# Half the up-projection row tiles of five chunks per layer by a 2x2 block scheme of seven products

## The chip, the cores and the metric

The kernel runs on one core of one Trainium2 chip. The metric is device time in microseconds of one execution: 2205.43 us, the median of three runs (2205.32 to 2205.55). TensorE (PE) multiplies, VectorE (DVE) and ScalarE (ACT) do elementwise work, SyncE (SP) issues the weight loads, and GpSimd (POOL) does little here. SBUF holds the working data. TensorE writes its results to PSUM, which has eight banks of 512 fp32 columns for each of the 128 partitions.

## What is computed

The reference is a trunk of two encoder layers over 256 tokens of width 2048, in fp32. Each layer has a mixer (layer 0: pooling and attention, layer 1: mLSTM; neither is touched here) and then the gated feed-forward part, which the change is about:

```python
x = x + conv_ffn(rms_norm(x, norm_ffn[layer]), w_up[layer], conv_w[layer], conv_b[layer], w_down[layer])

def conv_ffn(x, w_up, conv_w, conv_b, w_down):
    u = x @ w_up                                   # 256 x 2048 times 2048 x 11264
    up = jnp.pad(u, ((0, 0), (1, 1), (0, 0)))
    c = conv_w.astype(u.dtype)
    u = c[0] * up[:, :-2] + c[1] * up[:, 1:-1] + c[2] * up[:, 2:] + conv_b.astype(u.dtype)
    gate, val = jnp.split(u, 2, axis=-1)           # 5632 columns each
    return (jax.nn.silu(gate) * val) @ w_down      # 5632 x 2048
```

## The kernel before

**Products.** Every fp32 operand is used as two TensorE operands: a high half (the value rounded to the type that TensorE multiplies) and a low half (the rest). A product takes three matmuls: high x high, high x low, low x high. `mm` (line 203) issues each.

**Weights.** All weights come through one `Stream`. A load (SP queue, line 80) brings a 128 x 1024 fp32 tile of 512 KB into one of six raw buffers; `split` then makes the high half with a ScalarE cast (line 89) and the low half with a VectorE subtraction (line 90) into one of four "hl" buffers. The stream loads five tiles ahead of the tile in use and splits two ahead. A raw buffer is free again after its subtraction, an hl buffer after the last matmul that reads it.

**Feed-forward layer** (`ffn_layer`). The 5632 gate columns are 44 row tiles of 128 (with the 44 value tiles beside them), in chunks `FCH` of 4, 8, 8, 8, 8, 8 row tiles. `up` computes one row tile with the weights as the stationary operand and the 256 tokens moving: for each of 16 K tiles two 512-wide and two 256-wide matmuls (`stat_part`), into one buffer of the PSUM pool "mm" (two buffers of two banks). Then `gather` copies the one part out on ScalarE (line 366) and adds the other on VectorE (line 367), the norm's row scale R is multiplied in (line 890), and the conv, silu, gate and the split of the result into the chunk's tile `g` follow (lines 894 to 903, here called the tail). After a chunk's row tiles, `down` of the chunk before runs: for each of four column blocks of 512 a sum over that chunk's K tiles, with the activations stationary and the weights moving (`mov_part`, 512 wide, three terms, two token halves), into an "mm" buffer; `residual` adds it to x on VectorE (line 376). The second PSUM pool "ps" (four buffers of one bank) serves transposes.

**Order.** TensorE's order is the order in which the program is written. ScalarE's, VectorE's and SP's instructions are ordered by a scheduler before the run, and each engine then works through its own list from front to back. Small jobs beside the main line (norms, transposes) are generators in `Weave`, `wv`, which runs them at due times counted in estimated TensorE time (`wv.tick`).

```python
mmp = pool("mm", 2, space=PSUM)          # 2 x [128, 2, 512]
psp = pool("ps", 4, space=PSUM)          # 4 x [128, 512]
st = Stream(nc, wp, sp, weights, 5, 2)   # six raw buffers, four hl buffers
```

## Time and profile before

| | |
|---|---|
| runs, median of 3 | 2205.43 us (2205.32 to 2205.55) |
| profiled execution, span from first to last instruction | 2203.1 us (2.3 us under the median of the runs; no other time is listed for it) |
| mean granted TensorE clock | 1.000 |
| TensorE busy | 2197.9 us, 100% |
| VectorE busy | 1525.5 us, 69% |
| ScalarE busy | 1169.0 us, 53% |
| low halves of weights on VectorE (line 90) | 772, mean 1218 ns |
| casts of weights on ScalarE (line 89) | 771, mean 1047 ns |
| HBM traffic | 415.71 MB, mean 189 GB/s |

How to read it: rows give busy time, the mean of one instruction in ns and the idle time of the engine just before, with what ended it. Matmul rows overlap, as they are pipelined, so the pace of TensorE is read from the chain of waits in order of time (so many matmuls in so many us) and not from the mean of a matmul. A stage row gives busy time and, in brackets, the number of instructions for each engine, then the granted clock, the share of DMA time and the rate. Line numbers are those of the kernel before.

### The profile page before, as it was taken

The numbers are of one execution on the slowest core, as the hardware profiler recorded it, in microseconds if no ns is written. First come the engines' busy times: TensorE is split into PE (matmuls) and PEld (weight loads), VectorE is DVE, ScalarE is ACT, GpSimd is POOL, SyncE is SP. The second block draws the span as 40 slices with busy tenths as digits, with TensorE's granted clock in tenths as the row PEclk, the third lists the DMA queues.
The fourth block names the chain that finished last, engine by engine and source line by source line (L and its number), as shares of the span: only waits on it lengthen the run. The fifth ranks groups of instructions, "written<-read, shape, count | busy, mean of one in ns | idle before, by whom it ended". The sixth has DMA issues, their size and how long they took to land.

```text
span 2203.1 us, 30458 instructions
## 1 busy us (share of the span) xinstructions
PE 2197.9 (100%) x11616; PEld 1883.7 (86%) x11616; DVE 1525.5 (69%) x2172; ACT 1169.0 (53%) x1664; POOL 28.1 (1%) x40
## 2 busy tenths in 40 slices
PE   9999999999999999999999999999999999999999
PEld 8888888888888888889888888888888888888887
DVE  7686677776776767666767676667777677676764
ACT  7665555554554545456555454555555455454542
POOL 0020000000000000000000000000000000000000
PEclk9999999999999999999999999999999999999999
DMA  9555556556565666656565555556555656555664
GB/s 323 179 164 170 175 191 187 190 189 198 184 194 188 192 191 191 196 171 205 162 202 177 185 181 171 186 177 191 186 191 189 197 185 193 189 191 191 192 191 144
DMA packets 118036, 415.71 MB, mean 189 GB/s; under 512 B 13082, under 2 KB 15426, under 8 KB 117890
## 3 DMA queue, kind: packets, MB, share of 16 engines
q1 hardware_dynamic: 114656, 409.76, 58.2%
q10 hardware_dynamic: 3074, 3.75, 0.6%
q8 instruction: 91, 1.49, 0.3%
q14 instruction: 55, 0.45, 0.1%
q0 software_dynamic: 160, 0.26, 0.0%
HBM read 411.58 MB, written 2.14 MB: 188 GB/s over the span
## 4 chain that ended last, share of the span: by engine, by line
PE 100%; DVE 0%; issue 0%
PE up L203 45%; PE dn L203 21%; PE op L203 8%; PE mv L203 4%; PE mq L203 4%; PE mk L203 4%; PE mo L203 4%; PE qproj L203 3%; PE pool L203 1%; PE kproj L203 1%; PE vproj L203 1%; PE qk L203 1%; PE av L203 1%; PE end L203 0%; PE xt L254 0%; PE sc L203 0%
## 5 line engine op out<-in xcount | busy, mean ns | idle before, releaser
L90 DVE TENSOR_TENSOR hl<-w,hl 128x1024 fp32r<-128x1024 f32 (+2 forms) x772 | 939.1, 1218 | 466.6 <-ACT hl L89 464.8
L89 ACT CAST hl<-w 128x1024 fp32r<-128x1024 f32 (+1 forms) x771 | 806.9, 1047 | 677.3 <-PE dn L203 242.1
L203 PE MATMUL up<-xx,hl 128*128 128x512 f32 (+1 forms) x5632 | 984.2, 337 | 0.0
L203 PEld LDWEIGHTS up<-xx,hl 128*128 128x128 f32 x5632 | 857.9, 188 | 125.9
L203 PE MATMUL dn<-hl,g 128*128 128x512 f32 x2064 | 471.3, 389 | 0.0
L203 PEld LDWEIGHTS dn<-hl,g 128*128 128x128 f32 x2064 | 386.2, 188 | 79.5
L366 ACT COPY tb_up<-up 128x512 f32<-128x512 f32 x88 | 51.7, 587 | 154.0 <-PE up L203 154.0
L367 DVE TENSOR_TENSOR tb_up<-up,tb_up 128x512 f32<-128x512 f32 x88 | 60.8, 691 | 97.0 <-ACT tb_up L366 97.0
L894 ACT ACTIVATE y<-tb_up,cst 128x256 f32<-128x256 f32 x176 | 96.4, 595 | 47.0 <-DVE tb_up L890 47.0
L203 PE MATMUL mk<-xx,hl 128*128 128x512 f32 (+1 forms) x512 | 92.2, 337 | 0.0
L203 PE MATMUL mq<-xx,hl 128*128 128x512 f32 (+1 forms) x512 | 92.1, 337 | 0.0
L203 PE MATMUL mv<-hl,xx 128*128 128x512 f32 (+2 forms) x480 | 91.7, 350 | 0.0
L203 PE MATMUL op<-hl,cat 128*128 128x512 f32 x384 | 91.6, 393 | 0.0
L203 PE MATMUL mo<-hl,xx 128*128 128x512 f32 x384 | 90.4, 391 | 0.0
L203 PE MATMUL op<-hl,mcat 128*128 128x512 f32 x384 | 89.5, 392 | 0.0
L203 PEld LDWEIGHTS mq<-xx,hl 128*128 128x128 f32 x512 | 79.2, 188 | 11.6
L203 PEld LDWEIGHTS mk<-xx,hl 128*128 128x128 f32 x512 | 79.0, 188 | 11.4
L203 PEld LDWEIGHTS mv<-hl,xx 128*128 128x128 f32 x480 | 78.3, 189 | 11.2
L203 PEld LDWEIGHTS op<-hl,mcat 128*128 128x128 f32 x384 | 71.5, 188 | 14.6
L203 PEld LDWEIGHTS mo<-hl,xx 128*128 128x128 f32 x384 | 71.0, 188 | 14.2
L203 PEld LDWEIGHTS op<-hl,cat 128*128 128x128 f32 x384 | 70.9, 188 | 14.1
L895 DVE SCALAR_TENSOR_TENSOR y<-tb_up,cst,y 128x255 f32<-128x255 f32 x176 | 76.8, 478 | 0.0
(209 smaller groups left out, 1270.4 us busy)
## 6 DMA issues: line engine op xcount, KB each, us to landing
w<-in_up SPq DMA_DIRECT2D x352, 512.0 KB, 3.6
w<-in_dn SPq DMA_DIRECT2D x176, 512.0 KB, 4.1
w<-in_m_in SPq DMA_DIRECT2D x124, 512.0 KB, 4.1
w<-in_a_in SPq DMA_DIRECT2D x46, 512.0 KB, 4.4
w<-in_a_out SPq DMA_DIRECT2D x32, 512.0 KB, 3.4
w<-in_m_out SPq DMA_DIRECT2D x32, 512.0 KB, 3.5
w<-in_m_g SPq DMA_DIRECT2D x5, 432.0 KB, 3.4
x<-in_xn SPq DMA_DIRECT2D x4, 512.0 KB, 9.5
```

What stands on the lines that cost most here:

```text
L89: (self.nc.vector.tensor_copy if i + c == 0 else self.nc.scalar.copy)(hl[:, 0, c : c + n], w[:, c : c + n])
L90: self.nc.vector.tensor_sub(hl[:, 1, c : c + n], w[:, c : c + n], hl[:, 0, c : c + n].bitcast(F32))
L203: pe.matmul(out_, lhsT, rhs, start=start, stop=stop, skip_group_check=True)
L366: a.copy(tb, ps[:, :, 1, :])
L367: v.tensor_add(tb, ps[:, :, 0, :], tb)
L894: a.activation(y[:, j, :], u[:, j, :], AF.Identity, scale=cw(tl, 1), bias=cw(tl, 3))
L895: v.scalar_tensor_tensor(y[:, j, 1:S], u[:, j, 0 : S - 1], cw(tl, 0), y[:, j, 1:S], ALU.mult, ALU.add)
```

## The change

In chunks 1 to 5 of each layer (the five with eight row tiles), the last four of the eight row tiles are no longer computed one by one. With their value tiles they are 1024 output columns; these, the 256 tokens and each pair of K tiles are cut in two, so that each K pair is a 2x2 by 2x2 block product. Instead of eight block products of [128 tokens x 128] by [128 x 512] it takes seven, of sums of blocks: four activation sums (`sums`, once per layer, on VectorE from the already split activations) and weight sums made in `split` on VectorE in the raw buffers. The seven products are collected over the eight K pairs in six PSUM banks: one "mm" buffer (products 1 and 2 in the first bank, 3 in the second) and all four "ps" buffers. Weight tiles come in threes per K pair: "base", "one" (to which VectorE adds base) and "two" (whose halves VectorE adds to half of one and to each other), each feeding two products; four plain tiles per scheme finish the first output block. `decode` combines the banks on VectorE and ScalarE, `finish` transposes the result back to row tiles with TensorE and goes on with the unchanged tail. Per scheme 28 weight tiles are loaded and split where 16 were.

`_ffn_plan` writes TensorE's order by hand: row tiles in quarters, down blocks in slots of two K tiles, and the scheme's steps of one weight tile (six matmuls) between them. Down blocks of the chunk before now run between the row tiles of the chunk. From the feed-forward layer's start to its end the stream has one more raw and one more hl buffer, loads seven tiles ahead and splits three ahead.

```diff
+    def home(self, i, raw):
+        if self.more is None or i >= self.more[2]:
+            return self.wpool if raw else self.spool
+        return ((self.wpool if i % 7 < 6 else self.more[0]) if raw else
+                (self.spool if i % 5 < 4 else self.more[1]))
 
     def load(self, pieces=1):
         i = self.n_load
-        width = self.srcs[i].shape[-1]
+        src = self.srcs[i]
+        kind, src = src if isinstance(src, tuple) else ("plain", src)
+        width = src.shape[-1]
         n = width // pieces
-        w = self.wpool.tile([P, CH * P], F32, tag="w", name=f"w{i}")
+        w = self.home(i, True).tile([P, CH * P], F32, tag="w", name=f"w{i}")
         for c in range(0, width, n):
-            self.nc.sync.dma_start(w[:, c : c + n], self.srcs[i][:, c : c + n])
-        self.w[i] = w, n, width
+            self.nc.sync.dma_start(w[:, c : c + n], src[:, c : c + n])
+        self.w[i] = w, n, width, kind
         self.n_load += 1
 
     def split(self, then=None):
         i = self.n_split
-        w, n, width = self.w.pop(i)
-        hl = self.spool.tile([P, 2, CH * P], F32R, tag="hl", name=f"hl{i}")
+        w, n, width, kind = self.w.pop(i)
+        hl = self.home(i, False).tile([P, 2, CH * P], F32R, tag="hl", name=f"hl{i}")
+        if kind == "base":
+            self.base = w
+        if kind == "one":
+            self.one = w
+            self.nc.vector.tensor_add(w, w, self.base)
+        if kind == "two":
+            self.nc.vector.tensor_add(w[:, 0:512], w[:, 0:512], self.one[:, 0:512])
+            self.nc.vector.tensor_add(w[:, 512:1024], w[:, 512:1024], w[:, 0:512])
         for c in range(0, width, n):
             (self.nc.vector.tensor_copy if i + c == 0 else self.nc.scalar.copy)(hl[:, 0, c : c + n], w[:, c : c + n])
             self.nc.vector.tensor_sub(hl[:, 1, c : c + n], w[:, c : c + n], hl[:, 0, c : c + n].bitcast(F32))
...
-            def up(f, gt, i):
-                ps = stat_group(xx, list(range(KT)), f"up{layer}_{f}")
-                wv.until(lambda: norm.R is not None)
-                u = gather(tp, ps, f"up{layer}_{f}")
-                v.tensor_mul(u, u, bc(norm.R, 2))
...
+            def up(f, gt, i):
+                ps = mmp.tile([P, 2, 2, S], F32, tag="mm", name=f"up{layer}_{f}")
+                for q in range(KT // 4):
+                    stat_part(ps, xx, list(range(4 * q, 4 * q + 4)), q == 0, q == KT // 4 - 1)
+                    if q < KT // 4 - 1:
+                        yield
+                wv.until(lambda: norm.R is not None)
+                u = gather(tp, ps, f"up{layer}_{f}")
+                v.tensor_mul(u, u, bc(norm.R, 2))
+                tail(u, f, gt, i)
+
+            def sums():
+
+                vv = actp.tile([P, 2, KT // 2, S], F32, tag="B1", name=f"v{layer}")
+                for h in range(2):
+                    ks = slice(8 * h, 8 * h + 8)
+                    v.tensor_add(vv[:, 0], norm.xx[:, ks, 0, :].bitcast(F32), norm.xx[:, ks, 1, :].bitcast(F32))
+                    yield 5.0
+                    q = vv[:, 0].rearrange("p (a k) (t c) -> p a k t c", k=2, t=2)
+                    a11, a21, a12, a22 = (q[:, :, k, t, :] for k in range(2) for t in range(2))
+                    raw = vv[:, 1].rearrange("p k s -> p (k s)").rearrange("p (j a c) -> p j a c", j=4, a=4)
+                    s1, s2, s3, s4 = (raw[:, j] for j in range(4))
+                    v.tensor_sub(s1, a21, a22)
+                    v.tensor_add(s3, a11, a21)
+                    yield 3.0
+                    v.scalar_tensor_tensor(s2, s1, -1.0, a11, ALU.mult, ALU.subtract)
+                    v.tensor_sub(s4, s3, a12)
+                    v.tensor_sub(s4, s4, a22)
+                    yield 4.0
+                    for j in range(4):
+                        hi, lo = (sx[:, j, 4 * h : 4 * h + 4, i, :] for i in range(2))
+                        a.copy(hi, raw[:, j])
+                        v.tensor_sub(lo, raw[:, j], hi.bitcast(F32))
+                        yield 2.0
+
+            def product(bank, act, w, c, first, last):
+
+                (xh, xl), (wh, wl) = act, (w[:, j, c : c + 512] for j in range(2))
+                mm(bank, xh, wh, first, False)
+                mm(bank, xh, wl, False, False)
+                mm(bank, xl, wh, False, last)
+                wv.tick(0.68)
+
+            def block_of(k, t):
+                return [norm.xx[:, k, j, t * P : t * P + P] for j in range(2)]
+
+            def sum_of(j, p):
+                return [sx[:, j, p, i, :] for i in range(2)]
+
+            def quads(fs, gt, i0, name):
+
+                banks = {}
+                m = KT // 2
+                for p in range(m):
+                    ends = p == 0, p == m - 1
+                    for k in range(3):
+                        hl = st.next()
+                        if p == 0:
+                            if k == 0:
+                                two = mmp.tile([P, 2, 512], F32, tag="mm", name=f"p13_{name}")
+                                banks[1], banks[3] = two[:, 0], two[:, 1]
+                            else:
+                                for j in ((5, 7), (6, 4))[k - 1]:
+                                    banks[j] = psp.tile([P, 512], F32, tag="ps", name=f"p{j}_{name}")
+                        left = ((1, block_of(2 * p, 0)), (3, sum_of(3, p))), \
+                            ((5, sum_of(0, p)), (7, sum_of(2, p))), ((6, sum_of(1, p)), (4, block_of(2 * p + 1, 1)))
+                        for n, (j, act) in enumerate(left[k]):
+                            product(banks[j], act, hl, n * 512, *ends)
+                        if p == m - 1 and k == 0:
+                            c12 = cp1.tile([P, 512], F32, tag="c12", name=f"c12_{name}")
+                            a.copy(c12, banks[1])
+                        if p == m - 1 and k == 2:
+                            c12, c21, c22 = decode(banks, c12, name)
+                            wv.add(finish(c12, c22, fs[2:], gt, i0 + 2, name), 7.0)
+                        yield
+                for p in range(0, m, 2):
+                    hl = st.next()
+                    for n in range(2):
+                        product(banks[1], block_of(2 * (p + n) + 1, 0), hl, n * 512, False, p + n == m - 1)
+                    if p == m - 2:
+                        c11 = cp1.tile([P, 512], F32, tag="c11", name=f"c11_{name}")
+                        a.activation(c11, banks[1], AF.Copy, scale=norm.rcol[:, 0:1])
+                        wv.add(finish(c11, c21, fs[:2], gt, i0, name), 4.0)
+                    yield
+
+            def decode(banks, c12, name):
+
+                r1 = norm.rcol[:, 1:2]
+                c21 = cp1.tile([P, 512], F32, tag="c21", name=f"c21_{name}")
+                c22 = cp1.tile([P, 512], F32, tag="c22", name=f"c22_{name}")
+                v.tensor_add(c12, c12, banks[6])
+                v.tensor_add(c21, c12, banks[7])
+                a.activation(c21, c21, AF.Copy, scale=r1)
+                a.activation(c12, c12, AF.Copy, scale=n0)
+                v.scalar_tensor_tensor(c12, banks[3], n0, c12, ALU.mult, ALU.add)
+                v.scalar_tensor_tensor(c12, banks[5], n0, c12, ALU.mult, ALU.add)
+                v.scalar_tensor_tensor(c22, banks[5], r1, c21, ALU.mult, ALU.add)
+                v.scalar_tensor_tensor(c21, banks[4], r1, c21, ALU.mult, ALU.subtract)
+                return c12, c21, c22
+
+            def finish(top, bottom, fs, gt, i0, name):
+
+                for n, f in enumerate(fs):
+                    tr = psp.tile([P, 2, S], F32, tag="ps", name=f"tr{layer}_{f}")
+                    for j in range(2):
+                        for t, src in enumerate((top, bottom)):
+                            c = (2 * j + n) * P
+                            pe.transpose(tr[:, j, t * P : t * P + P], src[:, c : c + P], ident)
+                    u = tp.tile([P, 2, S], F32, tag="tb", name=f"tb_{layer}_{f}")
+                    a.copy(u, tr)
+                    tail(u, f, gt, i0 + n)
+                    yield 2.5
...
+            def down(c, gt, b):
...
+                for k in range(0, len(kts), 2):
+                    mov_part(ps, lambda k: gt[:, k], kts[k : k + 2], k == 0, k == len(kts) - 2)
+                    if k < len(kts) - 2:
+                        yield
+                residual(ps, b)
...
+            wv.add(sums_ready(), 8.0)
+            st.la, st.sa, st.more = 7, 3, (lp(f"fw{layer}", 1), lp(f"fh{layer}", 1), st.at + len(_ffn_plan()))
+            gts, run = {}, {}
+            for step in _ffn_plan():
+                kind, c = step[:2]
+                if kind != "d" and c not in gts:
+                    gts[c] = actp.tile([P, 8, 2, S], F32R, tag=f"B{c % 2}", name=f"g{layer}_{c}")
+                key = step[:3]
+                if key not in run:
+                    f0 = sum(FCH[:c])
+                    run[key] = (up(f0 + step[2], gts[c], step[2]) if kind == "n" else
+                                down(c, gts[c], step[2]) if kind == "d" else
+                                quads([f0 + 4 + j for j in range(4)], gts[c], 4, f"{layer}_{c}"))
+                next(run[key], None)
+            for e in run.values():
+                assert next(e, None) is None
+            st.la, st.sa, st.more = 5, 2, None
...
+def _ffn_plan():
+
+    plan = []
     for c, n in enumerate(FCH):
-        seq += [("u", u + i) for i in range(4 * n)]
-        u += 4 * n
+        whole = n - 4 if c else n
+        fill = [("n", c, i) for i in range(whole)]
         if c:
-            m = FCH[c - 1] // 4 * 8
-            seq += [("d", d + i) for i in range(m)]
-            d += m
-    m = FCH[-1] // 4 * 8
-    seq += [("d", d + i) for i in range(m)]
+            down = [("d", c - 1, b) for b in range(NB)]
+            fill = fill[:2] + down[:1] + fill[2:3] + down[1:2] + fill[3:] + down[2:]
+        slots = []
+        for e in fill:
+            slots += [e] * (4 if e[0] == "n" else FCH[e[1]] // 2)
+        if not c:
+            plan += slots
+            continue
+        m, late = KT // 2, c == len(FCH) - 1
+        here = [[] for _ in slots]
+        if c > 1:
+            for k in range(4):
+                here[k + 1].append(("s", c - 1, 0))
+        first, end = (0, len(slots)) if c == 1 else (8, len(slots)) if not late else (6, 24)
+        for k in range(3 * m):
+            here[first + k * (end - first) // (3 * m)].append(("s", c, 0))
+        if late:
+            for k in range(4):
+                here[end + k].append(("s", c, 0))
+        for e, extra in zip(slots, here):
+            plan += [e] + extra
+    for b in range(NB):
+        plan += [("d", len(FCH) - 1, b)] * (FCH[-1] // 2)
+    return plan
...
+def _quad_chunks(w):
+
+    out = []
+    for c in range(1, len(FCH)):
+        f = sum(FCH[:c]) + FCH[c] - 4
+        t = w.reshape(KT // 2, 2, P, 2, FT, P)[:, :, :, :, f : f + 4]
+        t = t.reshape(KT // 2, 2, P, 2, 2, 2, P).transpose(0, 1, 4, 2, 3, 5, 6).reshape(KT // 2, 2, 2, P, 512)
+        b11, b12, b21, b22 = (t[:, k, n] for k in range(2) for n in range(2))
+
+        def two(l, r):
+            return np.concatenate([l, r], axis=2)
+
+        out.append(np.stack([two(b11, b22), two(b12, b12), two(b22, b21)], axis=1))
+        out.append(two(b21[0::2], b21[1::2])[:, None])
```

71 lines of the change are left out of this document (43 added, 28 removed).

## The prediction, made before the run

> **What bounds the kernel now.** I read the page first, then the chain of waits in order of time, then one steady stretch of the feed-forward layer (eight up-projection row tiles and four down blocks) by engine, by group and instruction by instruction.
>
> The page: the span, busy time by engine, granted clock, traffic, the chain's share by engine.
>
> ```profile
> span 2203.1 us, 30458 instructions
> ...
> PE 2197.9 (100%) x11616; PEld 1883.7 (86%) x11616; DVE 1525.5 (69%) x2172; ACT 1169.0 (53%) x1664; POOL 28.1 (1%) x40
> ...
> PEclk9999999999999999999999999999999999999999
> ...
> DMA packets 118036, 415.71 MB, mean 189 GB/s; under 512 B 13082, under 2 KB 15426, under 8 KB 117890
> ...
> PE 100%; DVE 0%; issue 0%
> ```
>
> TensorE sets the time everywhere, at full clock. What a piece of it costs stands in the chain of waits (start, us, what):
>
> ```profile
> 1425.73 0.44 PE xt L254 x4
> ...
> 545.71 89.16 PE up L203 x512
> 634.87 43.53 PE dn L203 x192
> ```
>
> One up row tile is 89.16/8 = 11.145 us (64 matmuls, half of them 256 wide); a 512-wide matmul with the activation as weights is 43.53/192 = 0.2267 us; four transposes are 0.44 us.
>
> The same stretch by engine, then VectorE's groups and ScalarE's cast (busy, mean ns, idle before; the first row gives PE, PEld, DVE, ACT and POOL busy, clock, DMA share, GB/s):
>
> ```profile
> 545.70:678.40 132.70, 132.70 (x706) 113.85 (x705) 91.24 (x120) 68.02 (x88) 0.00 (x0) 1.00 0.60 191
> ...
> L90 DVE TENSOR_TENSOR hl<-w,hl 128x1024 fp32r<-128x1024 f32 x48 | 58.7, 1222 | 30.7 <-ACT hl L89 30.7
> L897 DVE SCALAR_TENSOR_TENSOR y<-tb_up,cst,y 128x255 f32<-128x255 f32 x16 | 7.0, 478 | 0.0
> ...
> L367 DVE TENSOR_TENSOR tb_up<-up,tb_up 128x512 f32<-128x512 f32 x8 | 5.5, 692 | 8.8 <-ACT tb_up L366 8.8
> L376 DVE TENSOR_TENSOR x<-x,dn 128x512 f32<-128x512 f32 x8 | 5.1, 684 | 1.6 <-PE dn L203 1.6
> ...
> L89 ACT CAST hl<-w 128x1024 fp32r<-128x1024 f32 x48 | 50.4, 1050 | 43.7 <-PE dn L203 23.6 <-PE up L203 20.1
> ```
>
> VectorE has 41.5 us of room in 132.7. Its instructions overlap a little at their ends, so I price them by the distance between starts, from the timeline (VectorE, then the one ScalarE row):
>
> ```profile
> 558.83 1.22 DVE L90 TENSOR_TENSOR hl<-w,hl 128x1024 fp32r<-128x1024 f32 x1
> 559.97 0.87 DVE L895 SCALAR_TENSOR_TENSOR y<-tb_up,cst,y 128x255 f32<-128x255 f32 x2
> 560.76 0.87 DVE L897 SCALAR_TENSOR_TENSOR y<-tb_up,cst,y 128x255 f32<-128x255 f32 x2
> ...
> 579.79 0.69 DVE L367 TENSOR_TENSOR tb_up<-up,tb_up 128x512 f32<-128x512 f32 x1 [1.10 <-ACT tb_up L366]
> 580.52 0.69 DVE L890 TENSOR_TENSOR tb_up<-tb_up,R 128x512 f32<-128x512 f32 x1
> 581.13 1.22 DVE L90 TENSOR_TENSOR hl<-w,hl 128x1024 fp32r<-128x1024 f32 x1
> ...
> 579.17 0.59 ACT L366 COPY tb_up<-up 128x512 f32<-128x512 f32 x1 [1.74 <-PE up L203]
> ```
>
> 1024 columns take 1.14 us, 512 take 0.61 (0.73 when the next one needs the result), two 255-column conv steps 0.79; a 256-column one I take at 0.34. The third up tile ends at 545.71 + 33.44 = 579.15; its bank pair is free when the add at 579.79 ends, 1.33 us later. Today nobody waits, since the other pair takes over.
>
> **The change, term by term.** *TensorE.* Ten times (five K chunks, two layers) four up row tiles go: 4 x 11.145 = 44.58 us. In come 8 K pairs x 7 products x 3 terms = 168 512-wide matmuls, 38.09, priced by the down rows since the operands stand the same way round, and 16 transposes to turn the result back, 1.76. Net -4.73 each, -47.3 us in all. Were nothing else to change, the profiled span would be 2203.1 - 47.3 = 2155.8; the runs lie 2.3 us above the span (2205.43 against 2203.1).
>
> *VectorE*, per chunk of that 132.7 us: 28 weight tiles in place of 16, so 12 more low halves at 1.14 = +13.7; eight sums "one" of 1024 columns, +9.1; eight "two" of 512 and, dependent, 512, 8 x 1.34 = +10.7; decoding, six operations of about 0.65, +4.0; four gathers and scalings gone, -5.3. 91.2 + 32.2 = 123.4 us against TensorE's new 128.0: from 69% to 96%. *ScalarE*: 12 more casts of 1.05 and a few copies, 68 + 15 = 83 us, no bound.
>
> *What becomes of PSUM.* The scheme holds one "mm" pair and all four "ps" banks from its first product to its decoding. An up tile or down block in between has only the other pair, and the next one may start only when VectorE has emptied it. Between two such groups TensorE has one scheme step of six matmuls, 1.36 us, which just covers the 1.33 us above, but only if VectorE stands ready. VectorE works in the order written into the program. That order, in the changed program, is what the following counts use; numbers are weight tiles.
>
> *First stretch of a middle chunk (third to fifth)*, from the residual add of the previous down column 3 to that of the new column 0. TensorE: 8 scheme steps 10.9, two up tiles 22.3, a down block of four slots 10.9, transposes 1.8: 45.9 us. VectorE must pass, ahead of that second residual: 20 low halves 22.8; a residual add 1.3; decoding 4.0; the tails of four scheme tiles 4 x 2.26 (two conv pairs, gate product, low half) and of two plain tiles 2 x 3.6 (with gather and scaling), 16.2; three "one" 3.4; two "two" 2.7: 50.4 us. So the next up tile, which needs the bank pair, is at least 4.5 us late, whatever lead the weights have.
>
> *Loads.* The order puts each "one" close behind the low half that frees its raw buffer (seven tiles before): for example tile 231's sum stands three 256-column operations and one low half (2.2 us) behind tile 224's low half. The load takes longer:
>
> ```profile
> DMA to landing us min/median/max: 3.3/3.7/4.5
> ```
>
> So VectorE, being late, also waits up to 1.5 us there. Walking the queue through one middle chunk with 3.8 us from release to landing gives TensorE waits of 0.8 (second up tile), 2.1 (first product of the new scheme) and 2.7 (the up tile after column 0): 5.6. The rest of the chunk has 82.1 us of TensorE against 70.4 of VectorE; there the walk leaves waits of 0.1 to 1.3 at four boundaries, 2.4. Together 8.0 per middle chunk, so 128.0 + 8.0 = 136 against 132.7.
>
> The Trainium skill, "DMA: Bandwidth & Descriptors", section "Anatomy of one DMA", fits 2.0 us plus bytes over 436 GB/s (for transfers GpSimd issues), an estimate of 3.2 us for these 512 KB. The row of this trace is longer and decides; by the page each of those waits would be about 0.5 us shorter and the total some 8 us lower.
>
> *Other chunks.* First chunk: the activation sums are two adds of 2048 columns (2.2 each), ten of 512 and eight low halves (0.61 each), 15.4 us, ahead of the first gather; with its other work VectorE reaches the weights of the third tile after about 27 us, TensorE after 23.4, less a small lead: 3 us. Second chunk: 97.6 us of TensorE, 90.6 of VectorE with fourteen sums to wait for, no first stretch: between 0 and 10; I take 5. Last chunk: the scheme starts two slots earlier, so the first stretch holds four low halves and one "two" more, 50.4 + 5.9 = 56.3 against 51.3 (four scheme steps more), then looser stretches: 5.0 at least, 9 taken. Attention, mLSTM and the last down chunk are untouched.
>
> *Sum.* Per layer 3 + 5 + 3 x 8 + 9 = 41 us of waits; two layers 82; 2203.1 - 47.3 + 82 + 2.3 = 2240 us. Bounds per layer: below 0 + 0 + 3 x 4.5 + 5 = 18.5 (VectorE's work alone), total 2195; above, the second rival.
>
> A page's rule speaks against the change by itself. The Trainium skill, "Perfetto Trace Analysis", section "Optimizing Tensor Performance", wants independent matmul groups to rotate through PSUM banks, so that emptying one overlaps the next. The 1.33 us row agrees on the cost, but the step between the groups covers it here unless VectorE is late; by the rule alone, eight uncovered boundaries a chunk would be 10.6 us, near the forecast.
>
> **The rivals.** *Slower than before is wrong: VectorE is not late.* Place: the residual add of each chunk's first down column. If the sums' loads land in time (VectorE's other waits use up the 1.5 us) and the leftovers of the previous stretch give it a lead, only the 4.5 and 5 us bounds stay: 2195. For it: VectorE's total is still under TensorE's, 123.4 to 128.0. Against: its order leaves 50.4 us to do in 45.9. It decides once that work fits 45.9, 9% less; then waits vanish and the time goes down to 2158 to 2165.
>
> *Loads slow down.* Each scheme adds 12 tiles of 0.524 MB, in all 415.7 + 62.9 = 479 MB, and in the dense stretches two tiles per 4.1 us, 256 GB/s. At the start of the run, where traffic is dense, a load lands late (rate, then kind and time to landing):
>
> ```profile
> DMA packets 6364, 17.58 MB, mean 352 GB/s; under 512 B 673, under 2 KB 801, under 8 KB 6361
> ...
> w<-in_a_in SPq DMA_DIRECT2D x23, 512.0 KB, 8.0
> ```
>
> Between 3.7 at 191 GB/s and 8.0 at 352, 256 gives 5.4. Then two sums of a first stretch wait 1.7 longer each and the looser stretches lose about 2: +5.4 per middle chunk, some 25 per layer, 2290. Against: those first loads queue many at a time, here at most a few are under way.
>
> *The change does less than it says:* the 512-wide products could take the up rows' time per column instead (11.145 us for 24,576 columns, 0.232 per 512): 39.0 per scheme, 9 us more in all, 2249, inside the forecast's range.
>
> **Chances.** Forecast, waits outgrow the saving (2210 to 2268): 0.62. Late only by VectorE's work, or not at all (2158 to 2201): 0.16. Slow loads (over 2268): 0.16. A tie, where the two cancel: 0.06. The measurement tells about 0.2%, 4.4 us, from no change: faster 0.16, same 0.06, slower 0.78. The likeliest gives 2240. The range reaches from VectorE's work bound, 2195, to where the slow loads begin to tell, 2280; it leaves out the wholly hidden case and the worst of the slow loads.
>
> **What would show it.** Right: VectorE at 90% or more in the middle chunks; TensorE with gaps of 2 to 3 us twice per chunk, ended by VectorE's residual add and gather; in the list of waits, weight sums waiting for loads; a middle chunk of about 136 us; transposes and products at 0.11 and 0.227 us each. Wrong: chunks near 128 us (VectorE was never late), gaps ended by casts or by DMA rather than by PSUM (then weights, not banks, are short), or a granted clock below 1.0.

## The result and the profile after

The changed kernel takes 2350.5 us (median of four runs, 2346.9 to 2356.9) against 2205.45: a ratio of 1.066, with an interval from 1.064 to 1.068. The direction was forecast, the size was not: +145 us against +35, and outside the range of 2195 to 2280.

From the page of the changed kernel, the lines that answer to those of before (span, busy time by engine, granted clock, traffic, the chain's share by engine):

```profile
span 2350.2 us, 29972 instructions
...
PE 2221.7 (95%) x10896; PEld 1846.9 (79%) x10896; DVE 1858.6 (79%) x2554; ACT 1323.7 (56%) x1840; POOL 29.2 (1%) x40
...
PEclk9999999999999999999999999999999999999899
...
DMA packets 135317, 478.59 MB, mean 204 GB/s; under 512 B 15002, under 2 KB 17346, under 8 KB 135170
...
PE 60%; DVE 20%; DMA 12%; issue 6%; ACT 2%; DVEq 0%; ACTq 0%
```

No engine is full: TensorE has gaps, VectorE is at 79%, and the chain, all TensorE before, now runs through VectorE and the loads for a third. The work is as counted. In the chain of the changed kernel, by time, a scheme step of six products and four transposes back (start, us, what):

```profile
571.32 1.37 PE p L220 x6
...
580.69 0.44 PE tr L1027 x4
```

The scheme itself is priced right (1.36 and 0.44 in the forecast). The loss lies in waits. The first feed-forward layer, cut at the residual add of each chunk's last down column (first chunk, second, third to fifth, last with the last down columns), by engine, then clock, DMA share and rate:

```profile
256.10:317.70 61.60, 50.94 (x283) 44.20 (x281) 52.36 (x80) 33.91 (x50) 0.71 (x1) 0.92 0.47 150
317.70:427.60 109.90, 101.03 (x476) 82.78 (x476) 92.35 (x114) 58.99 (x71) 0.00 (x0) 0.97 0.68 216
427.60:571.40 143.80, 133.39 (x634) 108.78 (x634) 121.56 (x155) 82.68 (x105) 0.00 (x0) 0.99 0.69 219
571.40:713.10 141.70, 133.02 (x633) 108.60 (x632) 121.22 (x154) 82.60 (x104) 0.00 (x0) 0.99 0.71 223
713.10:854.00 140.90, 132.99 (x633) 108.77 (x632) 121.67 (x154) 82.63 (x104) 0.00 (x0) 0.99 0.71 224
854.00:1059.10 205.10, 191.25 (x894) 156.42 (x893) 168.75 (x227) 122.80 (x171) 0.31 (x1) 0.98 0.64 202
```

Against TensorE's work alone (46.6, 97.6, three times 128.0, 182.8) these are 15, 12, 16, 14, 13 and 22 us too long: 92 in this layer and, by difference, 102 in the other. The forecast had 3, 5, 8, 8, 8 and 9. So no single place failed; every stretch loses 1.6 to 5 times what was allowed. In the second layer the middle chunks take 141.2, 145.5 and 145.1 us, 13 to 17.5 too long; the last two of them:

```profile
1848.30:1993.80 145.50, 134.65 (x633) 109.64 (x633) 121.94 (x155) 82.91 (x105) 0.00 (x0) 0.98 0.68 217
1993.80:2138.90 145.10, 134.87 (x633) 109.84 (x632) 121.59 (x154) 82.65 (x104) 0.00 (x0) 0.98 0.67 218
```

Who TensorE waits for, and VectorE for loads (the list of waits of the changed kernel, TensorE's rows and two of VectorE's: us in total, times, longest):

```profile
PE dn L220 <- DVE tb_up L384: 28.2, 22, 3.4
PE npr L220 <- DVE n L1086: 21.3, 2, 10.7
PE up L220 <- DVE x L393: 21.0, 15, 2.4
PE p L220 <- DVE tb_up L384: 14.9, 8, 2.6
PE up L220 <- DVE tb_up L384: 10.5, 10, 1.8
...
DVE w L101 <- DMA w<-in_qm: 61.2, 55, 4.6
...
DVE w L103 <- DMA w<-in_qm: 25.2, 29, 2.4
```

Lines 384 (gather) and 393 (residual add) are where VectorE empties the one PSUM pair left to plain groups: 74.6 us in these rows. The `npr` row is the norm of the feed-forward input, 10.7 us in each layer, which the forecast did not have. The last two rows are weight sums waiting for their own loads, 86.4 us. The middle chunk from 571 to 713, split where the forecast split it:

```profile
571.36:625.20 53.84, 49.23 (x243) 40.22 (x242) 50.18 (x76) 36.10 (x54) 0.00 (x0) 0.97 0.65 200
625.20:713.10 87.90, 83.83 (x392) 68.38 (x391) 71.08 (x80) 46.54 (x51) 0.00 (x0) 1.00 0.75 237
```

First stretch: VectorE busy 50.18 (50.4 counted), but 53.84 long (45.9 + 5.6 forecast). Rest: 87.90 (82.1 + 2.4). VectorE's work was right, its idle time and what follows from it was not.

And the clock drops. Around 606 us (windows of 3.4 us, same columns, clock before the DMA share; then TensorE's timeline):

```profile
605.30:608.70 3.40, 1.13 (x6) 0.59 (x4) 3.12 (x4) 2.40 (x5) 0.00 (x0) 0.99 0.42 143
608.70:612.10 3.40, 3.08 (x7) 2.48 (x8) 3.40 (x8) 0.14 (x1) 0.00 (x0) 0.50 0.56 170
612.10:615.50 3.40, 3.40 (x16) 2.77 (x15) 3.40 (x7) 2.86 (x5) 0.00 (x0) 1.00 0.50 155
```

```profile
603.54 2.89 PE L220 MATMUL dn<-hl,g 128*128 128x512 f32 x12
609.02 1.62 PE L220 MATMUL p<-hl,xx 128*128 128x512 f32 x3 [2.59 <-DVE tb_up L384]
```

A wait of 2.59 us ends at 609.02, and from 608.70 on TensorE has half speed for 3.4 us. The mean clock of the run is 0.980, or 47 us' worth of 2350; what that costs is asked below. Of the 194 us that TensorE loses, 123 are idle time; its busy time is 71 us longer than forecast (2221.7 us against 2197.9 - 47.3), which is where work at half speed would show. The Trainium skill, "TensorE: Matmul & The Clock Gate", section "HAM oscillation — how this bites in real kernels", warns of idle gaps over about 3.4 us. The half rate that it gives agrees with this trace (0.50), but here a wait of 2.59 us was enough, and half speed lasted 3.4 us where its example has about 1.67.

### The profile page after: what moved, and what is told of

Same layout as the page of the kernel before. It is cut to its first block, busy times and chain, and to the rows that moved or that the text cites. A ratio compares the mean times of both kernels' runs of the same rounds, so it can differ in the third digit from the quotient of the medians.

```text
span 2350.2 us, 29972 instructions
## 1 busy us (share of the span) xinstructions
PE 2221.7 (95%) x10896; PEld 1846.9 (79%) x10896; DVE 1858.6 (79%) x2554; ACT 1323.7 (56%) x1840; POOL 29.2 (1%) x40
## 4 chain that ended last, share of the span: by engine, by line
PE 60%; DVE 20%; DMA 12%; issue 6%; ACT 2%; DVEq 0%; ACTq 0%
PE dn L220 12%; DMA w<-in_qm 12%; DVE hl L107 10%; PE up L220 9%; PE op L220 7%; PE p L220 6%; PE mv L220 4%; PE mq L220 4%; PE mk L220 4%; PE mo L220 4%; PE qproj L220 3%; ACT hl L106 1%; DVE y L912 1%; DVE y L910 1%; DVE tb_up L384 1%
## 5 line engine op out<-in xcount | busy, mean ns | idle before, releaser
L106 ACT CAST hl<-w 128x1024 fp32r<-128x1024 f32 (+2 forms) x891 | 929.8, 1048 | 703.5 <-PE dn L220 191.2
L107 DVE TENSOR_TENSOR hl<-w,hl 128x1024 fp32r<-128x1024 f32 (+2 forms) x892 | 1077.7, 1218 | 287.7 <-ACT hl L106 280.8
L220 PE MATMUL up<-xx,hl 128*128 128x512 f32 (+1 forms) x3072 | 578.9, 343 | 35.7 <-DVE x L393 21.0
L220 PEld LDWEIGHTS up<-xx,hl 128*128 128x128 f32 x3072 | 495.2, 191 | 129.9 <-ACT hl L106 18.6
L220 PE MATMUL dn<-hl,g 128*128 128x512 f32 x2064 | 520.7, 404 | 42.4 <-DVE tb_up L384 28.2
L220 PEld LDWEIGHTS dn<-hl,g 128*128 128x128 f32 x2064 | 395.6, 194 | 146.8 <-DVE tb_up L384 35.1
L220 PE MATMUL p<-hl,sx 128*128 128x512 f32 x960 | 263.2, 398 | 0.0
L220 PE MATMUL p<-hl,xx 128*128 128x512 f32 x720 | 205.6, 402 | 23.7 <-DVE tb_up L384 14.9
L220 PEld LDWEIGHTS p<-hl,sx 128*128 128x128 f32 x960 | 177.9, 191 | 35.8
L220 PEld LDWEIGHTS p<-hl,xx 128*128 128x128 f32 x720 | 131.6, 191 | 51.7 <-issue 16.2
L101 DVE TENSOR_TENSOR w<-w,w 128x1024 f32<-128x1024 f32 x80 | 98.0, 1224 | 64.2 <-DMA w<-in_qm 61.2
L220 PE MATMUL mk<-xx,hl 128*128 128x512 f32 (+1 forms) x512 | 92.2, 337 | 0.0
L220 PE MATMUL mq<-xx,hl 128*128 128x512 f32 (+1 forms) x512 | 92.1, 337 | 0.0
L220 PE MATMUL mv<-hl,xx 128*128 128x512 f32 (+2 forms) x480 | 91.7, 350 | 0.0
L220 PE MATMUL op<-hl,cat 128*128 128x512 f32 x384 | 91.6, 393 | 0.0
L220 PE MATMUL mo<-hl,xx 128*128 128x512 f32 x384 | 90.4, 391 | 0.0
L220 PE MATMUL op<-hl,mcat 128*128 128x512 f32 x384 | 89.5, 392 | 0.0
L220 PEld LDWEIGHTS mq<-xx,hl 128*128 128x128 f32 x512 | 79.2, 188 | 11.6
L220 PEld LDWEIGHTS mk<-xx,hl 128*128 128x128 f32 x512 | 79.0, 188 | 11.4
L220 PEld LDWEIGHTS mv<-hl,xx 128*128 128x128 f32 x480 | 78.3, 189 | 11.2
L220 PEld LDWEIGHTS op<-hl,mcat 128*128 128x128 f32 x384 | 71.5, 188 | 14.6
L220 PEld LDWEIGHTS mo<-hl,xx 128*128 128x128 f32 x384 | 71.0, 188 | 14.1
```

The lines of the kernel that those rows point to most:

```text
L101: self.nc.vector.tensor_add(w, w, self.base)
L106: (self.nc.vector.tensor_copy if i + c == 0 else self.nc.scalar.copy)(hl[:, 0, c : c + n], w[:, c : c + n])
L107: self.nc.vector.tensor_sub(hl[:, 1, c : c + n], w[:, c : c + n], hl[:, 0, c : c + n].bitcast(F32))
L220: pe.matmul(out_, lhsT, rhs, start=start, stop=stop, skip_group_check=True)
```

## Experiments

Each kernel ran beside the kernel before on the same chip (medians of 2205.4 to 2205.6 us). Ratios are to that. A difference between two changed kernels compares medians of separate rounds, and the four runs of a kernel spread over 2 to 12 us, so a few us between two of them are not clear of noise. The kernels with an eighth raw buffer, with ScalarE emptying PSUM, and with sums that do not wait for loads also let the tile `c11` share the place of `c12`, to make room; what that costs was not measured.

**Activation sums behind the norm**

```diff
+ unit = xsp.tile([P, 1], F32, tag="unit", name=f"unit{layer}")
+ v.tensor_scalar(unit, norm.R[:, 0:1], 0.0, 1.0, ALU.mult, ALU.add)
...
- v.tensor_add(vv[:, 0], norm.xx[:, ks, 0, :].bitcast(F32), norm.xx[:, ks, 1, :].bitcast(F32))
+ v.scalar_tensor_tensor(vv[:, 0], norm.xx[:, ks, 0, :].bitcast(F32), unit,
+                        norm.xx[:, ks, 1, :].bitcast(F32), ALU.mult, ALU.add)
```

> The changed kernel, but the activation sums (sums) may start only once the norm's row scale R is there. What it tells apart: in the changed kernel the first up tile of layer 0 reaches its gather at 282.2 us against 269.3 before, 12.9 us late, with TensorE standing before the small matmul of the norm. If the activation sums stand ahead of the norm's chain in VectorE's order and cause it, that gather comes back to within 1 us of 269.3, the waits of that matmul (21 us in the two layers) go to nearly 0, and the time falls by 20 to 30 us to about 2325. If instead the sums are just too much work for the first chunk, wherever they stand, the 12.9 us appear again at the second or third tile and the time stays within 8 us of 2350.

2330.1 us, ratio 1.057 [1.055, 1.059]: 20 less. In the changed kernel VectorE's timeline has the sums (936 to 952) ahead of the operand that the norm needs (311):

```profile
257.48 2.28 DVE L936 TENSOR_TENSOR v<-xx 128x2048 f32<-128x2048 f32 x1
...
270.88 2.29 DVE L936 TENSOR_TENSOR v<-xx 128x2048 f32<-128x2048 f32 x1
...
276.23 0.48 DVE L311 TENSOR_SCALAR dg<-cst,re_n 128x128 f32<-128x128 f32 x2
```

With the edit TensorE runs through (timeline of this experiment):

```profile
265.90 0.60 PE L220 MATMUL npr<-dg,cst 128*128 128x256 f32 x2
266.15 34.02 PE L220 MATMUL up<-xx,hl 128*128 128x512 f32 x193
```

The first scheme starts at 308.7 in place of 318.5, and part of the 21.3 us won comes back as longer waits for the gather. So of the first chunk's 15 us about 10 were a matter of order and not of amount.

**No weight sums**

```diff
- self.nc.vector.tensor_add(w, w, self.base)
- self.nc.vector.tensor_add(w[:, 0:512], w[:, 0:512], self.one[:, 0:512])
- self.nc.vector.tensor_add(w[:, 512:1024], w[:, 512:1024], w[:, 0:512])
```

> The changed kernel without the weight sums: the three additions per K pair are left out, so the products use unsummed weight tiles. VectorE loses 8 x 1.14 + 8 x 1.34 = 19.8 us of work per scheme and never waits for a load. If VectorE's lateness (work and loads together) is what the middle chunks lose, they go from 142 to between 128 and 133 us, and the time falls by some 90 to 120 us to about 2245. If the banks alone are the matter (six of eight held, whoever is late), the chunks stay above 137 and the time above 2300.

2255.8, ratio 1.023 [1.021, 1.024]: 95 less. Middle chunks take 134.1 us from scheme to scheme. So the sums, which this kernel leaves out, make up two thirds of the 145 us, but half of the 194 us of waits, and the kernel without them is still slower than the one before. The first stretch of its second middle chunk:

```profile
550.59:600.23 49.64, 47.20 (x241) 38.93 (x240) 44.73 (x68) 36.01 (x53) 0.00 (x0) 1.00 0.66 214
```

VectorE has 44.73 us of work there, less than TensorE's 45.9, and the stretch is still 3.7 us too long.

**Weight sums as work, but without waits for loads**

```diff
- self.nc.vector.tensor_add(w, w, self.base)
+ self.nc.vector.tensor_sub(self.junk, self.last, self.last)
...
+ self.last = hl[:, 1].bitcast(F32)
```

`self.last` is the low half made just before; the two 512-column sums are changed in the same way. The sums themselves are left out.

> The changed kernel, with each weight sum kept as work for VectorE (a subtraction of the same width) but taken from the low half made just before it, into a tile that nobody uses: so no sum waits for a load. Left out: the sums themselves, so the products are formed with wrong weights. e2, without that work and without its waits, took 2256. Theory 'it is the waits for loads at the sums that the forecast undersized' (86 us in all in the list of waits, about 9 per middle chunk): middle chunks fall from 141 to 133 to 134 and the time to about 2275. Rival 'the sums' own 20 us of work per chunk are what makes VectorE late, and the waits only fill its idle time': it stays at 2330 or more. Half of each: 2300.

2285.8, ratio 1.037 [1.035, 1.038]: 65 less, so about two thirds of the 95 are the waits for loads and 30 the work itself. But in the middle chunks of the first layer only 3 to 6 us go (137.8 and 138.7 us from scheme to scheme; 144.1 and 141.5 in the changed kernel), less than the 7 to 8 expected; the first such stretch gives 10, the last one, to the end of the layer, 6. In the second layer the three middle chunks, between the same residual adds, give 3, 8 and 8. The same stretch of the changed kernel has its loads landing so (min, median, max):

```profile
DMA to landing us min/median/max: 3.1/4.2/5.2
```

3.8 was used in the forecast, 0.4 less than this median.

**An eighth raw buffer**

```diff
- return ((self.wpool if i % 7 < 6 else self.more[0]) if raw else
+ return ((self.wpool if i % 8 < 6 else self.more[0]) if raw else
...
- st.la, st.sa, st.more = 7, 3, (lp(f"fw{layer}", 1), lp(f"fh{layer}", 1), st.at + len(_ffn_plan()))
+ st.la, st.sa, st.more = 8, 3, (lp(f"fw{layer}", 2), lp(f"fh{layer}", 1), st.at + len(_ffn_plan()))
```

> The changed kernel with one more raw buffer (eight; loads one tile further ahead; the c11 tile shares c12's place to make room). A tile's load is then issued about 2.2 us earlier relative to its sum. In the changed kernel VectorE's sums wait 61.2 + 25.2 = 86 us for loads. If these waits make VectorE late and so cost the time, most of them go (under 30 us left) and the time falls by 25 to 50 us to about 2310. If they only fall where VectorE would have waited for something else anyway, they go and the time stays within 12 us of 2350.

2377.7, ratio 1.077 [1.075, 1.079]: 27 more, where less was expected. The waits of sums for loads grew to 115 us (86.4 in the changed kernel). Timeline of VectorE, then of SyncE's queue:

```profile
633.39 1.23 DVE L107 TENSOR_TENSOR hl<-w,hl 128x1024 fp32r<-128x1024 f32 x1
634.78 1.23 DVE L107 TENSOR_TENSOR hl<-w,hl 128x1024 fp32r<-128x1024 f32 x1 [0.16 <-ACT hl L106]
639.60 1.23 DVE L101 TENSOR_TENSOR w<-w,w 128x1024 f32<-128x1024 f32 x1 [3.59 <-DMA w<-in_qm]
```

```profile
634.65 0.33 SPq L89 DMA_DIRECT2D w<-in_qm  x1
```

The low half that ends at 634.62 frees a buffer, the load into it goes out at 634.65, and the sum that ends VectorE's wait starts 4.95 us later, only one low half behind. Loads in this stretch land within 5.1 us, so it is this load that the sum waits for; and counting tiles, the next low half in VectorE's order is of a tile loaded six places earlier. At this place the planned order has the sum right behind the end of its load; the further buffer has moved the load and the sum forward together, and the sum waits with older low halves behind it. That this holds at the other places too is argued from the growth of the waits; here the buffer bought no slack.

**Sums tied behind the tile before** (in the kernel with all three edits below and in its variant with four schemes)

```diff
+ unit = self.units.tile([P, 1], F32, tag="behind", name=f"unit{self.n_split}")
+ self.nc.scalar.activation(unit, self.last, AF.Copy, scale=0.0, bias=1.0)
...
- self.nc.vector.tensor_add(w, w, self.base)
+ self.nc.vector.scalar_tensor_tensor(w, w, self.behind(), self.base, ALU.mult, ALU.add)
...
+ self.last = hl[:, 0, 0:1].bitcast(F32)
```

The first two lines are the body of `behind`; `self.last` is here a column of the high half of the tile before. The first of the 512-column sums is tied in the same way.

> The kernel of e7_late_empty_order, with every weight sum tied to the weight tile before it: the tile is multiplied by a 1 that ScalarE derives from the previous tile's high half, so the order that is planned can't place the sum ahead of that cast, and its load, issued seven low halves earlier, has landed by then. e7 has 55.8 us of VectorE waits for loads at sums and some 37 us between its span and the span of before less 47.3. Theory 'the planned order puts each sum where its load has not landed yet, and that is what is left': the waits for loads go, VectorE catches up in the last chunk, and the time falls by 10 to 25, to about 2177. Rival 'with the banks free those waits are harmless, and what is left is weights that come late because VectorE has too much to do in the last chunk': within 5 of e7, 2190 to 2199, or above it, since the small ScalarE operations (160 of them) and the two-input form add work.

> The same tie in the kernel of e9_four_schemes (2192), where the crowded last chunk is left out. TensorE's work is 37.8 us under the kernel before, so 2168 is the least. Theory of e12: TensorE's waits for low halves at products (7.3 us, and as much again in short ones in layer 1) go with the waits for loads, and it comes near 2175. Rival: 2188 to 2196.

2279.8, ratio 1.033 [1.032, 1.035], and 2245.5, 1.018 [1.017, 1.020]: 86 and 54 more than the kernels without the tie. No sum waits for a load any more, and the time went up and not down. The rival had allowed for a time above 2199, but from the added work; the waits show another reason. The list of waits of the first of the two (ScalarE's casts, then TensorE):

```profile
ACT hl L111 <- DVE w L106: 112.6, 49, 3.3
...
ACT hl L111 <- DVE w L109: 67.9, 39, 3.0
```

```profile
PE p L226 <- DVE hl L112: 27.6, 33, 3.0
PE p L226 <- ACT hl L111: 18.6, 9, 3.0
```

Now each cast waits for its sum (180 us) and each sum for the cast before: the two engines take turns, and TensorE waits for weights. By these rows the early place of the sums, which I had taken for the fault, is what lets ScalarE run ahead.

**Weight sums on GpSimd**

```diff
- self.nc.vector.tensor_add(w, w, self.base)
+ self.nc.gpsimd.tensor_add(w, w, self.base)
...
```

The two 512-column sums go there too.

> The changed kernel with all weight sums on GpSimd in place of VectorE. GpSimd's two-operand instruction of 256 columns took 0.84 to 1.21 us before, so 1024 columns should take 3.4 to 4.8 and one scheme's sixteen some 60 us of a 140 us chunk: it fits. VectorE loses the same 19.8 us per scheme as without the sums, and its waits for loads. By the theory that VectorE's lateness is the loss: 2245 to 2275, a little above the kernel without the sums, since the sums come later to the cast. Rival: GpSimd's sums come too late for the weights, or slow VectorE down beside them (VectorE's rows over 1.30 us in place of 1.22): over 2350.

2372.4, ratio 1.076 [1.074, 1.078]: 22 more. Groups of this experiment (busy, mean ns, idle before):

```profile
L107 DVE TENSOR_TENSOR hl<-w,hl 128x1024 fp32r<-128x1024 f32 (+2 forms) x892 | 1230.4, 1395 | 320.3 <-ACT hl L106 314.9
L101 POOL TENSOR_TENSOR w<-w,w 128x1024 f32<-128x1024 f32 x80 | 247.3, 3092 | 740.4 <-DMA w<-in_qm 472.3 <-DVE tb_up L384 126.4 <-DVE y L910 70.3
```

A sum takes 3092 ns there (1224 on VectorE), and VectorE's low halves go from 1218 to 1395 ns on average. Over 892 of them that is 158 us, so three quarters of the 208 us of sums taken off VectorE come back as slower work on it. How much of the 22 us is this, and how much the sums' own slowness, was not told apart.

**ScalarE empties PSUM**

```diff
- u = gather(tp, ps, f"up{layer}_{f}")
+ em = cp1.tile([P, 2, 2, S], F32, tag="em", name=f"em_up{layer}_{f}")
+ a.copy(em, ps)
+ u = tp.tile([P, 2, S], F32, tag="tb", name=f"tb_up{layer}_{f}")
+ v.tensor_add(u, em[:, :, 0, :], em[:, :, 1, :])
...
+ em = cp1.tile([P, 2, 512], F32, tag="em", name=f"em_dn{layer}_{c}_{b}")
+ a.copy(em, ps)
- residual(ps, b)
+ residual(em, b)
```

> The changed kernel with the PSUM pairs of plain up tiles and down blocks emptied whole by ScalarE into SBUF (about 1.1 us each), VectorE adding from there: VectorE's work is the same, but a pair comes free without VectorE's turn. If the wait is for VectorE's place in its order (the step the prediction rests on), the TensorE waits at group boundaries shrink to ScalarE's copy, middle chunks go from 142 to 131 to 135 us and the time falls by 60 to 90 us, to about 2275. If VectorE's sheer work and its waits for loads are what counts, TensorE then waits for weight tiles instead and the time stays within 25 us of 2350.

2299.8, ratio 1.043 [1.041, 1.045]: 51 less. TensorE's waits for lines 384 and 393 are gone from the list, and another has grown:

```profile
PE dn L220 <- ACT g L917: 37.1, 8, 4.7
...
PE dn L220 <- DVE g L918: 16.1, 13, 2.0
```

The bank mechanism was real. Behind it stood the gate products of the scheme's own tiles, which the third slot of down block 0 needs before VectorE has come to them. Of the Trainium skill's "Perfetto Trace Analysis", section "Optimizing Tensor Performance" (independent groups should rotate through PSUM banks, so that emptying one overlaps the next), this run bears out the cost where they cannot: the same products and sums, with the one pair free sooner, take 51 us less.

**The same, with TensorE kept busy**: eighteen 512-wide products with zero weights ahead of that third slot, in four chunks per layer.

```diff
+ if b == 0 and k == 4 and c >= 1 and not last:
+     for _ in range(18):
+         mm(ps[:, 0], zero, norm.xx[:, 0:1].rearrange("p a b c -> p (a b c)"), False, False)
```

> The kernel where ScalarE empties, with 18 matmuls of 512 columns by a zero weight tile (they add nothing to the result) ahead of the third slot of each down block 0 of chunks 1 to 4, just where TensorE waits 4.7 us eight times and where the clock then runs at half speed for 10.2 us. 18 x 0.2267 = 4.1 us of filling that lies inside the wait. If the half clock is a cost of its own, caused by the wait, the half-clock time falls from 102 to about 25 us and the time by some 8 x 4 to 5 = 25 to 40 us, to about 2265, although TensorE has more to do. If the half clock costs nothing there (TensorE waits for VectorE anyway), the time stays within 8 us of 2300; if it doesn't come from the wait, the clock stays as it was.

2296.5, ratio 1.041 [1.040, 1.043]: 3 less, which the intervals do not tell from nothing. TensorE's timeline, first with ScalarE emptying alone, then with the extra products (`dn<-xx,zero`):

```profile
604.78 1.22 PE L220 MATMUL dn<-hl,g 128*128 128x512 f32 x2 [4.63 <-ACT g L917]
```

```profile
597.22 4.36 PE L220 MATMUL dn<-xx,zero 128*128 128x512 f32 x18
601.41 1.52 PE L220 MATMUL dn<-hl,g 128*128 128x512 f32 x6
604.79 0.73 PE L220 MATMUL dn<-hl,g 128*128 128x512 f32 x2 [1.86 <-ACT g L917]
```

The waiting products start at 604.78 and 604.79: the gate product comes when it comes, whatever TensorE does meanwhile. The mean clock rose from 0.978 to 0.986, 18 of some 50 us' worth, and the time fell by 3. So at this place the half clock is a consequence of VectorE's lag and costs little by itself. What the rest of it costs, and what it costs in the changed kernel itself, was not tested.

**Down blocks later**

```diff
- fill = fill[:2] + down[:1] + fill[2:3] + down[1:2] + fill[3:] + down[2:]
+ fill = fill[:3] + down[:2] + fill[3:] + down[2:]
```

> The changed kernel with the order of plain work changed alone: in each chunk three row tiles, then down blocks 0 and 1, the last row tile, down blocks 2 and 3 (before: two row tiles, block 0, the third, block 1, the fourth, blocks 2 and 3). Down block 0 needs the scheme tiles of the chunk before; their tails have one row tile (11 us) longer. If late tails of the scheme tiles are a large part of the loss, the time falls by 20 us or more. By the theory that VectorE's place in its order holds the banks, the tails wait less but the banks as much: within 15 us of 2350.

2332.0, ratio 1.058 [1.056, 1.060]: 19 less, between the two expectations, so this run alone does not decide between them. It is a few us in each stretch from scheme to scheme (143.0, 138.1 and 140.8 in place of 146.4, 144.1 and 141.5 in the first layer).

**Together**

> The first two edits of e7 without the third: activation sums behind the norm, and ScalarE emptying the PSUM pairs of plain groups; the order of down blocks as in the changed kernel. If the parts simply add, e4's 2300 less e1's 20 gives 2280, and the order is then worth 86 us on top, against 19 alone in e6: because with the banks free the longest wait left is TensorE's at the third slot of down block 0 for the gate products of the scheme's tiles (37 us in e4). If the order's gain does not hang on the banks, e11 lies near 2213 and parts do not add.

The first two of three edits (activation sums behind the norm, ScalarE emptying): 2270.1, ratio 1.029 [1.027, 1.030]. Near the 2280 of simple addition; the row `PE dn L220 <- ACT g L917: 37.1` is there unchanged.

> Three edits together: activation sums after the norm's scale, ScalarE empties the plain groups' PSUM pairs, down blocks later. In the kernel where ScalarE empties, TensorE still waits 53 us for tiles g of the scheme (37.1 + 16.1) and 21.3 at the norm, and runs 102 us at half clock. If the waits left there are these latencies, they go below 15 us and the half-clock time below 25 us, and the time falls from 2300 by 60 to 90 us to 2210 to 2240. If VectorE's total work (123 us a chunk) is the bound, chunks stay at 133 or more and the time above 2260.

All three: 2194.2, ratio 0.995 [0.993, 0.997], 0.5% faster than the kernel before. The order is worth 76 us here and 19 alone: the gate products are the longest wait only once the banks are free, and with all three edits they are gone from TensorE's list of waits. Two stretches of this kernel, in the first layer, scheme to scheme, then the last scheme to the end of the layer:

```profile
564.70:693.40 128.70, 128.70 (x634) 107.72 (x634) 119.62 (x155) 86.94 (x109) 0.00 (x0) 1.00 0.75 246
...
816.00:983.00 167.00, 160.15 (x742) 131.79 (x741) 139.41 (x188) 108.00 (x150) 0.31 (x1) 0.98 0.65 214
```

A middle chunk of the first layer now takes 128.7 us with TensorE busy throughout, against 128.0 worked out in the forecast (130.2 and 132.6 from scheme to scheme in the second layer), although over the run the weight sums still wait 55.8 us for loads. So in these chunks the waits for loads cost nothing once VectorE is no longer late for the other reasons.

> The kernel of e7_late_empty_order, with the scheme in four K chunks per layer in place of five: the last K chunk goes back to eight plain up row tiles. In e7 the middle chunks run at TensorE's own pace (128.6 and 128.7 us from scheme to scheme) and the loss that is left sits behind the last scheme's start: 167.0 us to the end of layer 0, with TensorE waits of 3.4, 2.5 and 2.2 us for low halves and a slot of the gate products. Theory 'the crowded last chunk is what eats the rest' (its 24 + 4 steps stand in 22 slots): leaving it out gives back 4.7 us of TensorE work per layer but wins about 13, so 2194 - 17 = 2177. Rival 'the waits belong to the last down column and to VectorE's lag from the chunks before': they stay, and the time goes up by 9 to 2203.

```diff
- whole = n - 4 if c else n
+ whole = n - 4 if c and not late else n
...
- for k in range(3 * m):
+ for k in range(0 if late else 3 * m):
```

2191.7, ratio 0.994 [0.992, 0.995]: the lowest median, but 2.5 us under the last one in place of 17, a difference that the intervals do not separate. 9.5 us of TensorE work came back, and the time above TensorE's own work fell from 17 to 6 us in the first layer, but only from 20 to 17 in the second, where products in the middle chunks wait up to 2.3 us for low halves. Why they do so in that layer and not in the first was not found out.

## Why the prediction was wrong

**Right: what the change does to TensorE.** -47.3 us: steps and transposes cost what was worked out, and in the first layer the middle chunk of the kernel with all three edits comes within 0.7 us of 128.0.

**Right: VectorE's work.** 121.2 to 121.7 us busy per middle chunk (123.4 forecast), 50.18 in the first stretch (50.4). The rest had 71.08; the 70.4 of the forecast does not follow from its own 123.4 - 50.4, which is 73.0, but no term of the sum rests on it. As the chunks were longer than forecast, VectorE's share in the first layer came to 85 to 86%, under the 90% named as a sign of being right.

**Right in kind: the one PSUM pair.** The two waits named, residual add and gather, make up 74.6 us of the 123 us in TensorE's list, and taking VectorE out of the emptying won 51 us.

**Wrong: "First chunk: ... 3 us"**. It measured 15. The step added up VectorE's work ahead of the first gather, but not where the norm's operand stands in it: TensorE waits 10.7 us for the norm, behind activation sums that nobody needs yet.

**Wrong: "Together 8.0 per middle chunk".** It measured 13 to 16 in the first layer and 13 to 17.5 in the second; in the chunk shown, 7.9 in the first stretch (5.6 forecast) and 5.8 in the rest (2.4). In the first layer there are three parts: loads took 4.2 us in place of 3.8, and removing all waits for loads wins 3 to 6; the sums' own work is about 4 (138 to 139 without the waits, 134 without the sums); and 6 are there without any sums at all, although VectorE's work then fits. Of these 6, TensorE's list for the second middle chunk without sums names 1.5 for a gate product of the scheme's tiles, a wait that the forecast did not have, and 0.8 for a gather; the rest was not placed. The forecast gives only the sums of its walk, so which of its steps in VectorE's queue fell short stays open.

**Wrong: "between 0 and 10; I take 5" and "9 taken"** for the second and the last chunk: 12 and 22. Neither was walked through: each was taken from totals of work; fourteen sums with no lead in the second chunk were called out and still taken at half of the bound.

**Not in the forecast as a cost: the clock.** Named only as a sign of being wrong. Half speed follows most waits of 1.8 us or more; the one place tested shows that it costs little there (3 us for 18 us' worth of clock). The first chunk and the rest were not tested, so a part of the 71 us of longer busy time may be a cost of its own.

**The rivals.** "VectorE is not late" and "products pay the up rows' price" fell. "Loads slow down" gave a time nearer the result, 2290, but not its reason: loads land in 4.2 us, not 5.4. "It decides once that work fits 45.9" fell: without the weight sums VectorE has 44.73 us in the first stretch, and TensorE still waits. With ScalarE emptying the banks, the activation sums behind the norm and the down blocks moved, the first layer's middle chunks have no waits at nearly the same VectorE work (119.62 us busy). So who empties the banks and the order of the work decided it there, and not 9% less work.

By parts, the 194 us of waits are not a sum of independent items: undoing the activation sums' order gives 20, the emptying 51, these two together 80, the order of down blocks alone 19, and all three 156.

## What to carry to other kernels

When an engine that follows its written order goes from 69% to 95% of the bottleneck's work, its total says little: ask at each handover what stands ahead of the one instruction that is waited for, in the first chunk and at the seams as well as in the steady one. Waits that share one late engine hide one another, so an edit that wins 19 us alone may win 76 once the wait in front of it is gone, and edits should be tried together before the idea is given up. Tying an instruction to a later point so as to stop it from blocking can cost more than the blocking, when another engine was living on its lead.

## What the runs showed of the hardware

- In the changed kernel TensorE's granted clock was at 0.50 during or just after 19 of the 24 waits of 1.5 us or more in the feed-forward layers. The shortest of the 19 is 1.80 us (ended at 955.93); a wait of 2.20 us (ended at 1885.69) had none. Around the 10.7 us wait for the norm, which ends at 276.86, the half clock lasted 10.2 us:

```profile
267.30:270.70 3.40, 0.00 (x0) 0.00 (x0) 3.40 (x7) 0.62 (x1) 0.00 (x0) 1.00 0.48 154
270.70:280.90 10.20, 4.04 (x12) 3.41 (x13) 9.41 (x19) 2.46 (x4) 0.00 (x0) 0.50 0.16 51
280.90:284.30 3.40, 3.40 (x21) 2.98 (x20) 2.08 (x3) 2.20 (x4) 0.00 (x0) 0.99 0.02 5
```

- 1024 columns added on GpSimd took 3092 ns against 1224 on VectorE, and VectorE's low halves took 15% longer on average over that run (1395 against 1218 ns).
- Loads of 512 KB landed in 4.2 us (median) at 200 to 240 GB/s, in 3.7 at 191.
